# The gate columns of the first window of a hybrid decoder layer: projected third instead of eighth

## The chip, the core and the metric

The kernel runs on one core of a Trainium2 chip. The metric is the device time of one execution in microseconds (us). The engines are called as in the profile: PE (TensorE, the matrix engine; PEld is its weight loads), DVE (VectorE), ACT (ScalarE), POOL (GpSimd) and SP (SyncE, which here issues nearly all DMAs). Each engine runs its own instructions strictly in the order in which they stand; between engines, semaphores make one wait for another.

## What is computed

One layer on 2048 prompt tokens (one sequence) and 8 x 4 sample tokens, with D = 1024, in fp32:

```python
h = rms_norm(x, attn_norm)
u, q, k, v, g, z = split(h @ w_in)            # 512, 256, 256, 512, 512, 16 columns
y5 = rms_norm(GLU(gelu(S5(u))))               # 32 groups of complex diagonal state space
logf = log_sigmoid(z @ w_gate_up + b_gate) / 16
# gated linear attention, 4 heads, chunks of 64 tokens, b = cumsum(logf)
qe = q * exp(b); ke = k * exp(-b)
att = tril(qe @ ke.T); o = att @ v + qe @ S   # S: the state carried from chunk to chunk
o = rms_norm(o) * silu(g)
x = x + concat(y5, o) @ w_o
h2 = rms_norm(x); a, b = split(h2 @ w_up)     # 2 x 2816 columns
x = x + (silu(causal_conv3(a)) * b) @ w_down
```

Every fp32 product is made of three products of split values (high times high, high times low, low times high), so a block of 128 x 128 weights costs three matmuls per tile of tokens.

## The kernel before

**Stages.** The prompt goes through the first half of the layer in four windows of 512 tokens (`for w in range(NWIN)`); window 1 also carries the 32 sample tokens, so its tiles of columns are 272 wide. After the last window, the ConvFFN runs over all tokens. In the profile window 0 is the stretch from 20 to 212.4 us, windows 1 to 3 run to about 831, and the ConvFFN follows.

**A window.** First z (16 columns) is projected, and a generator `gen_gla_pre` (L1348) makes from it the decay factors: absolute value, exp and log on ACT, a subtraction and two scans on DVE (`TENSOR_TENSOR_SCAN`), subtractions of the value in the middle of each chunk, and then two exponentials on ACT, E1 = exp(b/16) and E2 = exp(-b/16), 128 x 1024 each (`qe` and `ke` in the code). Then the blocks of `w_in` follow in the order that `PARTS(w)` (L607) gives. A number is a block of 128 columns, done by `channels(m)` with columns on partitions and 512 tokens along the row: one PSUM bank, 24 matmuls. Blocks 0 to 3 are u (the bank is copied out by ACT), 4 and 5 are q, 6 and 7 are k. DVE multiplies q into E1 and k into E2 in place (`SCALAR_TENSOR_TENSOR t_L<-mm,t_L` and `TENSOR_TENSOR t_L<-mm,t_L`); at block 4 the builder first writes out the rest of `gen_gla_pre`. "v" and "g" are parts of 512 columns done by `tokens(part)` with tokens on partitions: four PSUM banks at once, one for each tile of 128 tokens, filled in four steps of 24 matmuls, one for each of four weight blocks. A tile of v is copied out, and with it the generator of the gated attention of these 128 tokens starts (`gen_gla_tile`); a tile of g goes through Silu on ACT and then through a product with a gain on POOL. After the part "g", two generators `gen_hT` for the next window are added as well: they load the next 512 rows of x, normalise them (ACT for the squares, DVE for `t_L<-t_L,rr,gain`), and, once all parts of this window are through, transpose and split them. At the end of a window come the products with `w_o` for the gated half of the mix: 2 halves of the columns times 4 tiles of 12 matmuls, each of which needs the attention's output of its tile.

**Banks.** PSUM's banks 0 to 3 (`mm` in the rows) serve these projections in turn, banks 4 to 7 (`bg`) the background work. A projection waits for the bank that it takes to be emptied.

**Weights.** A block of 512 KB is loaded by a DMA on SP's queue, its high part made by ACT (or POOL), its low part by POOL or DVE (`TENSOR_TENSOR t_L<-t_L,t_L 128x1024`). A list made from `PARTS` (`specs`, L611) sets the order of the loads.

**Order of the work.** The program is written out once, when it is built. All else than the projections is made of generators with priorities; a planner with a clock of estimated times writes out pieces of them between the groups of matmuls (`bg.tick()`), or until a given generator is done (`bg.drain`). Apart from the above, one such generator makes S5's tables (`gen_tables`): powers and products of complex numbers on DVE, first 16 x 128 to 16 x 512 elements, then eight tables with 16 products of 128 x 144 and 128 x 128 and two additions each. Another writes the first ConvFFN inputs at the end of window 3: rows of x are normalised, transposed by PE (`<-ident`), and evicted by ACT with a gain (`t_L<-bg,fgainc`). All instructions are recorded by one helper line (L290), so that the rows tell them apart by tiles: `mm`, `bg` and `all` are PSUM banks, `t_L`, `t_H` and `pair_L` slots of SBUF that serve all kinds of data, `decay` the decays of whole chunks, `rr` the reciprocal norms.

Of the kernel before, what the change touches and what calls it, by code (L numbers as in the profile page):

```python
# [29 lines left out]
NWIN = TP // WT  # L30
# [395 lines left out]
def kernel(ctx: ExitStack, tc: tile.TileContext, ins, outs):  # L426
# [179 lines left out]

    def PARTS(w):  # L607

        return (0, 1, 4, 5, 6, 7, "v", "g", 2, 3) if w < NWIN - 1 else (0, 1, 2, 3, 4, 5, 6, 7, "v", "g")

    specs = []  # L611
    swap = set()
    for w in range(NWIN):
        for part in PARTS(w):
            if isinstance(part, str):
                specs += [wrows(w_in, k, 1024 if part == "v" else 1536) for k in (0, 2, 4, 6)]
                continue
            if part < 4:
                swap.add(len(specs))
            specs.append(wcols(w_in, part * P))  # L620
        specs += [wrows(w_o, k, n * 512) for n in range(2) for k in (4, 6)]
# [1361 lines left out]
    for w in range(NWIN):  # L1983
# [100 lines left out]
        for part in PARTS(w):  # L2084
            if not isinstance(part, str):
                channels(part)
                continue
            if smp:
                BANKS.update(mm=(0, 5), bg=(5, 3))
            tokens(part)  # L2090
            if smp:
                BANKS.update(mm=(0, 4), bg=(4, 4))
                if part == "g":
                    S.put(xsamp.pop())
            if part == "g":
                if w + 1 < NWIN:
                    for pair in range(2):
                        hT[w + 1, pair] = bg.add(0, gen_hT(w + 1, pair))
                    if w + 1 == SW:
                        hT["s"] = bg.add(0, gen_hT_sample())  # L2100
# [610 lines left out]
```

## Time and profile before

| | |
|---|---|
| median of 3 runs | 2420.09 us (2413.03 to 2422.62) |
| the profiled execution | 2419.89 us, span 2418.2 us |
| mean granted clock of PE | 0.971 of full speed |
| PE busy | 2282.5 us (94%) |
| DVE busy | 1545.2 us (64%) |
| ACT busy | 896.8 us (37%) |
| POOL busy | 539.0 us (22%) |
| queue of the loads and stores | 357.53 MB, 47.0% of the 16 DMA engines |

Busy is the time in which an engine worked on an instruction; 94% for PE means that 135.7 us of the span are left in which no matmul ran. A share over the whole span does not tell where these are, so the rows below go by stretches and by waits.

### The profile page before, as it was taken

To read this page: it belongs to the slowest core of one execution; us is meant where nothing else is said; L and a number is where in the kernel's file an instruction comes from. 1 tells how busy PE (TensorE), PEld (TensorE's weight loads), DVE (VectorE), ACT (ScalarE), POOL (GpSimd) and SP (SyncE) were. 2 spreads that over 40 slices of the span, in tenths; PEclk is the share of its full clock that TensorE was granted. 3 is DMA by queue.
4 is the path that set the end of the run, shared out by engine and by line. 5 is a ranking of instruction groups with operands and counts; after the bars stand their busy time and mean duration, and the time that the engine had idled before them with its cause. 6 is when DMAs were issued, how large, how long until landed. Compare 5 with 4: busy or idle time off the path is not lost.

```text
span 2418.2 us, 32048 instructions
## 1 busy us (share of the span) xinstructions
PE 2282.5 (94%) x11809; PEld 1933.0 (80%) x11809; DVE 1545.2 (64%) x2743; ACT 896.8 (37%) x1634; POOL 539.0 (22%) x645
## 2 busy tenths in 40 slices
PE   7798999999999899999998998999999998999998
PEld 5577877777787689999998997887888776777776
DVE  6777547866633467654436655666666778686887
ACT  3243144434422453243233113344443435343444
POOL 5245425546432435631010010000000000000011
PEclk9899999999999999999999999999999999999999
DMA  6124546426653723344544752222222478676754
GB/s 170 62 94 132 149 121 196 115 83 200 174 168 112 252 93 106 114 143 121 168 166 142 249 177 62 68 81 87 79 79 79 147 232 267 226 247 215 242 184 151
DMA packets 357021, 359.72 MB, mean 149 GB/s; under 512 B 56546, under 2 KB 274842, under 8 KB 356864
## 3 DMA queue, kind: packets, MB, share of 16 engines
q1 hardware_dynamic: 356512, 357.53, 47.0%
q8 instruction: 93, 1.52, 0.3%
q14 instruction: 64, 0.52, 0.1%
q10 hardware_dynamic: 352, 0.15, 0.0%
HBM read 250.99 MB, written 106.62 MB: 148 GB/s over the span
## 4 chain that ended last, share of the span: by engine, by line
PE 61%; DVE 16%; ACT 6%; issue 4%; POOL 3%; DMA 1%; SPq 0%; ACTq 0%; DVEq 0%; POOLq 0%
PE all L290 42%; DVE t_L L290 13%; PE mm L290 11%; PE bg L290 8%; ACT t_L L290 5%; DVE t_H L290 2%; DVE pair_L L290 2%; POOL t_H L290 1%; POOL t_L L290 1%; POOL pair_L L290 1%; DMA t_L<-in_w_o_dram 0%; ACT t_H L290 0%; ACT pair_L L290 0%; DMA t_L<-Wd 0%; SPq L290 0%
## 5 line engine op out<-in xcount | busy, mean ns | idle before, releaser
L290 PE MATMUL all<-t_L,t_L 128*128 128x512 f32 (+4 forms) x7358 | 1472.2, 361 | 51.0 <-DVE t_L L290 20.0
L290 PEld LDWEIGHTS all<-t_L,t_L 128*128 128x128 f32 (+2 forms) x7358 | 1280.0, 189 | 236.4 <-DVE t_L L290 36.0
L290 DVE TENSOR_TENSOR t_L<-t_L,t_L 128x1024 fp32r<-128x1024 f32 (+9 forms) x636 | 553.0, 896 | 175.5 <-ACT t_L L290 116.3
L290 ACT ACTIVATE t_L<-t_L 128x1024 fp32r<-128x1024 f32 (+8 forms) x450 | 361.9, 825 | 440.8 <-DVE t_L L290 360.3
L290 PE MATMUL mm<-t_L,t_L 128*128 128x512 f32 (+2 forms) x2160 | 491.5, 384 | 15.4 <-DVE t_L L290 12.3
L290 PEld LDWEIGHTS mm<-t_L,t_L 128*128 128x128 f32 (+1 forms) x2160 | 382.6, 191 | 100.5 <-issue 17.5
L290 POOL TENSOR_SCALAR rr<-ss 128x1 f32<-128x1 f32 (+1 forms) x51 | 19.7, 386 | 1044.7 <-ACT pair_L L290 955.2
L290 DVE TENSOR_TENSOR t_L<-t_L,all 128x512 f32<-128x512 f32 (+2 forms) x268 | 172.4, 643 | 101.8 <-PE all L290 37.9
L290 POOL TENSOR_SCALAR t_L<-t_L 128x1024 fp32r<-128x1024 f32 (+1 forms) x91 | 117.4, 1298 | 320.5 <-PE all L290 146.7
L290 POOL TENSOR_TENSOR t_L<-t_L,t_L 128x1024 fp32r<-128x1024 f32 x49 | 136.3, 2784 | 51.8 <-ACT t_L L290 39.6
L290 ACT ACTIVATE t_L<-all 128x512 f32<-128x512 f32 (+2 forms) x134 | 71.6, 539 | 191.0 <-PE all L290 186.1
L290 DVE TENSOR_TENSOR t_L<-t_L,pair_L 128x512 f32<-128x512 f32 (+2 forms) x138 | 93.4, 679 | 56.4 <-ACT pair_L L290 51.4
L290 ACT ACTIVATE pair_L<-all 128x512 f32<-128x512 f32 (+1 forms) x104 | 61.6, 593 | 154.1 <-PE all L290 134.1
L290 PE MATMUL bg<-t_L,t_L 128*128 128x256 f32 (+7 forms) x628 | 111.2, 344 | 2.3 <-DVE t_H L290 2.3
L290 DVE SCALAR_TENSOR_TENSOR t_L<-all,cw,t_L 128x351 f32<-128x351 f32 (+1 forms) x132 | 74.7, 566 | 48.0 <-ACT t_L L290 47.2
L290 PEld LDWEIGHTS bg<-t_L,t_L 128*128 128x128 f32 (+4 forms) x628 | 85.1, 183 | 24.6 <-issue 10.8
L290 ACT ACTIVATE t_L<-all,cw 128x352 f32<-128x352 f32 x66 | 42.4, 642 | 147.1 <-PE all L290 130.2
L290 ACT ACTIVATE t_L<-bg 128x512 fp32r<-128x512 f32 (+7 forms) x121 | 53.5, 461 | 103.8 <-PE bg L290 99.3
L290 DVE SCALAR_TENSOR_TENSOR t_L<-t_L,cw,t_L 128x1024 f32<-128x1024 f32 x44 | 56.5, 1285 | 24.6 <-ACT t_L L290 23.8
L290 ACT ACTIVATE junk<-bg 128x128 bf16<-128x128 f32 (+1 forms) x68 | 18.8, 276 | 120.5 <-PE bg L290 118.9
L290 ACT ACT_TABLE_LOAD x41 | 52.6, 1283 | 23.0 <-DVE t_L L290 14.7
L290 DVE TENSOR_TENSOR t_L<-pair_L,t_L 128x144 f32<-128x144 f32 (+5 forms) x107 | 54.6, 538 | 8.2 <-ACT pair_L L290 5.8
(180 smaller groups left out, 1643.4 us busy)
## 6 DMA issues: line engine op xcount, KB each, us to landing
t_L<-in_w_up_dram SPq DMA_DIRECT2D x88, 512.0 KB, 4.9
t_L<-x2d SPq DMA_DIRECT2D x80, 512.0 KB, 5.9
t_L<-in_w_in_dram SPq DMA_DIRECT2D x64, 512.0 KB, 5.5
x2d<-t_L SPq DMA_DIRECT2D x48, 512.0 KB, 3.1
gT<-t_L SPq DMA_DIRECT2D x44, 512.0 KB, 2.7
t_L<-gT SPq DMA_DIRECT2D x48, 384.0 KB, 4.8
t_L<-in_w_down_dram SPq DMA_DIRECT2D x34, 512.0 KB, 4.9
t_L<-in_w_o_dram SPq DMA_DIRECT2D x24, 512.0 KB, 5.5
```

Of the source, the lines that this page charges most:

```text
L290: r = fn(*args, **kw)
```

## The change

`PARTS` gives window 0 an order of its own: "g" stands third, behind the u blocks 0 and 1, instead of eighth. Windows 1 to 3 keep theirs.

```diff
     def PARTS(w):

-        return (0, 1, 4, 5, 6, 7, "v", "g", 2, 3) if w < NWIN - 1 else (0, 1, 2, 3, 4, 5, 6, 7, "v", "g")
+        return (0, 1, "g", 4, 5, 6, 7, "v", 2, 3) if w == 0 else (0, 1, 4, 5, 6, 7, "v", "g", 2, 3) if w < NWIN - 1 else (0, 1, 2, 3, 4, 5, 6, 7, "v", "g")
```

The matmuls stay the same. The weight loads follow the new order, the two generators for window 1's rows are added after the third part instead of the eighth, and the planner, whose clock now sees other waits, writes out the background work at other places all through the first third of the program. Three places show it.

ACT, in window 0, around E1 and E2. Before (`t_L_453` and `t_L_454` are E1 and E2, `t_L_319` one of S5's 16-partition arrays, `decay_412` the decays):

```order
L290 ACTIVATE decay_412<-decay_412 128x16
L290 ACTIVATE t_L_319<-t_L_319 16x128
L290 ACT_TABLE_LOAD
L290 ACTIVATE t_L_319<-t_L_319 16x128 x2
L290 ACT_TABLE_LOAD
L290 ACTIVATE t_L_453<-t_L_409 128x1024
L290 ACTIVATE t_L_454<-t_L_409 128x1024
L290 ACTIVATE t_L_633<-t_L_585 128x1024
```

With the change (E1 and E2 are `t_L_480` and `t_L_481`, and `mm_403` to `mm_406` are g's four tiles):

```order
L290 ACTIVATE decay_439<-decay_439 128x16
L290 ACTIVATE t_L_480<-t_L_436 128x1024
L290 ACTIVATE t_L_481<-t_L_436 128x1024
L290 ACTIVATE t_L_319<-t_L_319 16x128
L290 ACT_TABLE_LOAD
L290 ACTIVATE t_L_319<-t_L_319 16x128 x2
L290 ACT_TABLE_LOAD
L290 ACTIVATE pair_L_557<-mm_403 128x512
L290 ACTIVATE pair_L_557<-mm_404 128x512
L290 ACTIVATE pair_L_580<-mm_405 128x512
L290 ACTIVATE pair_L_580<-mm_406 128x512
L290 ACTIVATE t_L_599<-t_L_545 128x1024
```

E1 and E2 moved up before S5's operations, and the four Silus stand behind all of them; the first matmul of block 4 waits for the first Silu, since it takes that bank.

DVE, where blocks 4 to 7 are multiplied into E1 and E2. Before (`mm_457`, `mm_489`, `mm_521`, `mm_553` are the four blocks):

```order
L290 SCALAR_TENSOR_TENSOR t_L_453<-mm_457,t_L_453 128x512
L290 SCALAR_TENSOR_TENSOR t_L_453<-mm_489,t_L_453 128x512
L290 TENSOR_TENSOR t_L_454<-mm_521,t_L_454 128x512
L290 TENSOR_TENSOR t_L_454<-mm_553,t_L_454 128x512
L290 TENSOR_TENSOR pair_L_437<-t_L_432 16x128
```

With the change (`mm_603`, `mm_677`, `mm_722`, `mm_762`; the rows with `rr` are normalisations of window 1's rows, those of 16 partitions S5's tables, of which the first and the last of a run are shown):

```order
L290 TENSOR_TENSOR t_L_513<-t_H_517,pair_L_320 16x512
L290 SCALAR_TENSOR_TENSOR t_L_480<-mm_603,t_L_480 128x512
L290 SCALAR_TENSOR_TENSOR t_L_616<-t_L_616,rr_622,gain 128x1024
...
L290 SCALAR_TENSOR_TENSOR t_L_480<-mm_677,t_L_480 128x512
L290 COPY t_L_514<-t_L_512 16x128
...
L290 SCALAR_TENSOR_TENSOR t_L_626<-t_L_626,rr_667,gain 128x1024
L290 TENSOR_TENSOR t_L_481<-mm_722,t_L_481 128x512
L290 TENSOR_TENSOR t_H_517<-t_L_514 16x256
...
L290 TENSOR_TENSOR t_L_515<-t_H_517,pair_L_320 16x512
L290 TENSOR_TENSOR t_L_481<-mm_762,t_L_481 128x512
```

The four products stood together and are now spread: three normalisations between the first two, eight operations on S5's arrays and two normalisations between the second and the third, twelve operations on S5's arrays between the third and the last. The first of the four also stands behind a whole block of S5's operations that it stood ahead of before.

PE, at the end of window 3, where the `w_o` products end and the ConvFFN begins. Before (`bg` and `all` rows are transposes of the first ConvFFN inputs, `all_7073` the first FFN product):

```order
L290 MATMUL mm_6916<-t_L_6815,t_L_6719 128x512
L290 MATMUL bg_6932<-ident,t_L_6767 128x128 x4
L290 MATMUL bg_6945<-ident,t_L_6767 128x128 x4
L290 MATMUL bg_6984<-ident,t_L_6769 128x128 x4
L290 MATMUL bg_6997<-ident,t_L_6769 128x128 x4
L290 MATMUL all_7045<-ident,t_L_6771 128x128 x4
L290 MATMUL all_7058<-ident,t_L_6771 128x128 x4
L290 MATMUL all_7073<-t_L_6734,t_L_6821 128x352
```

With the change, two pieces with 30 matmuls between them (`mm_6828`, `mm_6948` and `mm_7001` are `w_o` products):

```order
L290 MATMUL mm_6828<-t_L_6612,t_L_6726 128x512
L290 MATMUL bg_6844<-ident,t_L_6789 128x128 x4
L290 MATMUL bg_6857<-ident,t_L_6789 128x128 x4
L290 MATMUL mm_6897<-t_L_6660,t_L_6688 128x512
...
L290 MATMUL mm_6948<-t_L_6883,t_L_6718 128x512
L290 MATMUL bg_6963<-ident,t_L_6791 128x128 x4
L290 MATMUL bg_6976<-ident,t_L_6791 128x128 x4
L290 MATMUL mm_7001<-t_L_6660,t_L_6726 128x512
```

The transposes of the first two tiles moved in between the last `w_o` products; all of them stood behind the last of these before.

## Rows read from the trace of the kernel before

**Rows 1.** The page's first part: busy us, share of the span, instructions.
```profile
PE 2282.5 (94%) x11809; PEld 1933.0 (80%) x11809; DVE 1545.2 (64%) x2743; ACT 896.8 (37%) x1634; POOL 539.0 (22%) x645
```
**Rows 2.** Stretches: length, busy us of PE, PEld, DVE, ACT, POOL (instructions), PE clock, DMA share, GB/s.
```profile
100.00:140.00 40.00, 37.82 (x207) 28.25 (x205) 12.20 (x45) 7.61 (x32) 6.02 (x7) 0.83 0.15 53
831.00:848.00 17.00, 5.71 (x28) 4.16 (x26) 7.62 (x21) 15.90 (x38) 7.37 (x12) 0.64 1.03 356
20.00:212.40 192.40, 165.42 (x762) 127.37 (x761) 142.62 (x266) 60.32 (x114) 83.87 (x58) 0.88 0.35 101
212.40:831.00 618.60, 596.06 (x3294) 475.30 (x3293) 354.45 (x672) 226.50 (x508) 265.75 (x277) 0.97 0.51 151
```
**Rows 3.** Waits of PE from 20 to 212.4 us: total us, times, longest us.
```profile
PE bg L290 <- DVE pair_L L290: 11.8, 2, 8.2
PE mm L290 <- DVE t_L L290: 10.7, 1, 10.7
```
**Rows 4.** PE's timeline in window 0: start, us, operation, count, [idle before <-releaser].
```profile
44.62 16.51 PE L290 MATMUL mm<-t_L,t_L 128*128 128x512 f32 x70 [1.25 <-POOL t_L L290]
...
71.84 22.53 PE L290 MATMUL mm<-t_L,t_L 128*128 128x512 f32 x84 [10.71 <-DVE t_L L290]
...
104.85 0.49 PE L290 MATMUL bg<-t_H,t_H 128*128 128x128 f32 x2 [2.18 <-DVE t_H L290]
...
157.68 2.79 PE L290 MATMUL bg<-ident,pair_L 128*128 128x128 f32 x12 [3.59 <-DVE pair_L L290]
...
203.01 1.09 PE L290 MATMUL bg<-ident,pair_L 128*128 128x128 f32 x4 [8.23 <-DVE pair_L L290]
```
**Rows 5.** ACT's timeline in window 0.
```profile
64.52 0.31 ACT L290 ACTIVATE t_L<-t_L 16x128 f32<-16x128 f32 x1 [7.95 <-DVE t_L L290]
64.84 1.28 ACT L290 ACT_TABLE_LOAD   x1
...
66.66 1.28 ACT L290 ACT_TABLE_LOAD   x1
67.96 4.85 ACT L290 ACTIVATE t_L<-t_L 128x1024 f32<-128x1024 f32 x5
...
147.26 0.60 ACT L290 ACTIVATE t_H<-mm 128x512 f32<-128x512 f32 x1
```
**Rows 6.** DVE's timeline in window 0 and the first microseconds of window 1.
```profile
58.65 4.26 DVE L290 TENSOR_TENSOR t_L<-t_L,pair_L 128x512 f32<-128x512 f32 x2
...
71.03 1.27 DVE L290 SCALAR_TENSOR_TENSOR t_L<-mm,t_L 128x512 f32<-128x512 f32 x2
...
73.42 4.78 DVE L290 TENSOR_TENSOR pair_L<-t_L 16x128 f32<-16x128 f32 x2
...
82.28 0.75 DVE L290 TENSOR_TENSOR pair_L<-t_L 16x256 f32<-16x256 f32 x2
...
88.08 0.68 DVE L290 TENSOR_TENSOR t_L<-pair_L 16x512 f32<-16x512 f32 x1
...
88.96 0.47 DVE L290 TENSOR_TENSOR pair_L<-t_L 16x128 f32<-16x128 f32 x2
...
171.71 4.86 DVE L290 SCALAR_TENSOR_TENSOR t_L<-t_L,rr,gain 128x1024 f32<-128x1024 f32 x4
...
189.88 1.30 DVE L290 TENSOR_TENSOR t_L<-pair_L,t_L 128x144 f32<-128x144 f32 x2
...
213.17 0.52 DVE L290 TENSOR_TENSOR t_L<-pair_L,t_L 128x144 f32<-128x144 f32 x2
...
217.20 0.69 DVE L290 TENSOR_TENSOR t_H<-t_H,t_H 128x512 f32<-128x512 f32 x1
```
**Rows 7.** POOL's timeline beside DVE's block from 73.42: low parts of weights.
```profile
70.98 7.07 POOL L290 TENSOR_TENSOR t_L<-t_L,t_L 128x1024 fp32r<-128x1024 f32 x3 [8.61 <-ACT t_L L290]
```
**Rows 8.** PE's timeline where the ConvFFN begins.
```profile
835.36 1.59 PE L290 MATMUL bg<-ident,t_L 128*128 128x128 f32 x8 [2.86 <-ACT t_L L290]
...
842.60 1.97 PE L290 MATMUL all<-ident,t_L 128*128 128x128 f32 x8 [5.65 <-ACT t_L L290]
```

## The prediction, made before the changed kernel was run

> **What bounds the kernel now.** I read five views, from coarse to fine. The page's first part says that TensorE (PE) is busy for 2282.5 of the span's 2418.2 us [rows 1]: a change that only reorders can win back PE's idle time and nothing else, so I look for idle time that this change can reach. The table of stretches gives it: the first window of 512 tokens (20 to 212.4 us) has 192.40 - 165.42 = 27.0 us without PE work, while the three other windows together (212.4 to 831 us) have 618.60 - 596.06 = 22.5 us in more than three times the length [rows 2]. The waits of PE in the first window name who ends that idle time, and VectorE (DVE) ends nearly all of it: 10.7 us once before a projection, 11.8 us in two waits of the output side [rows 3]. PE's timeline places them [rows 4]. The first projections end at 44.62 + 16.51 = 61.13; the next matmul starts at 71.84, 10.71 us later, on a DVE release. Smaller waits follow at 104.85 (2.18) and 157.68 (3.59), and a larger one at 203.01 (8.23). Window 1 begins at 212.4.
>
> The wait at 61 is this one. Block 4 (q) is multiplied by the decay factors E1, block 6 (k) by E2; until DVE has done that, the four banks stay full, and "v", the next part, needs all four. DVE reads E1 and E2 at 71.03 [rows 6]; ScalarE (ACT) has made them in the five operations from 67.96, behind one 16x128 operation at 64.52 and two table loads [rows 5]. So PE stands behind a chain DVE scan, DVE subtractions (58.65, ended at 62.9), ACT, DVE.
>
> **The change, part by part** (+ is time lost; the sum is made against the profiled execution, 2419.89 us, which lies 0.2 us under the median of 2420.09).
>
> (a) *Removed: the wait before v.* Parts 0, 1 and "g" together have as many matmuls as 0, 1, 4, 5, 6, 7, so PE still runs without a pause to 61.13, and the next thing it meets is now block 4, not v. Block 4 needs an empty bank only, not E1. **-10.7**. With it goes the 2.18 wait at 104.85, on the first tile of the gated attention, which v now feeds later: **-2.2**.
>
> (b) *Added: block 4 waits for g's first bank.* g's four banks are emptied by Silu on ACT, and the order shows Silu behind E1, E2, the 16x128 operations and two table loads. DVE's subtractions end at 62.9 [rows 6]; E1 and E2 take 4.85 / 5 = 0.97 each [rows 5], to 64.85; then the operations and table loads that take from 64.52 to 66.66 + 1.28 = 67.94, 3.4 us, to 68.2; the first Silu takes 0.60 [rows 5], to 68.8. PE waits from 61.1 to 68.8: **+7.7**. Bounds: 6 if one table load overlaps the subtractions' end, 9.5 if the small DVE operations that feed the 16x128 ones slip by 2 us. On this the Trainium skill speaks against the change: "ScalarE: Activation LUTs", section What ACT_TABLE_LOAD costs, puts 1.28 us of load and some 1.38 us of drain on each switch of table. By it two switches would hold Silu 2.8 us longer, the wait would be 10.5 and the whole sum below -1.1. The rows do not show the drain: the load at 66.66 is followed by work at 67.96, right at its end [rows 5], so I keep 7.7.
>
> (c) *Added: v waits for blocks 4 to 7 all the same, later.* Before, DVE does their four products back to back at 71.03. Now each waits for its own matmuls, and the order puts between them a block of the S5 tables' 16-partition operations, twelve more of them later, and the five normalisations of window 1's rows, which come early because "g" sets them free. When is the last of the four done? Blocks 4 to 7 are 96 matmuls, 22.53 / 84 = 0.268 us each just after a pause [rows 4], so they run from 68.8 to 94.5, and v's fourth tile wants its bank 18 matmuls later, at 99.4. The first table block took from 73.42 to 88.08 + 0.68 = 88.76 before, 15.3 us [rows 6]; now it starts at 71, with a weight subtraction of about 1.2 in it, so DVE comes to block 4's product at 87.5. A product takes 1.27 / 2 = 0.63, a normalisation 4.86 / 4 = 1.2 [rows 6]: block 4's is done at 88.1, three normalisations at 91.7, block 5's at 92.3, eight small operations (0.47 / 2 each, 1.9) and two normalisations at 96.6, block 6's at 97.3, twelve table operations (as from 82.28 to 88.76, 6.5 [rows 6]) at 103.8, block 7's at 104.4. PE waits 104.4 - 99.4 = **+5.0**. Bounds: 0 if the first table block runs undisturbed (its 16x128 pair then takes 0.47 instead of 4.78 [rows 6]), 12 if the normalisations and the second block run at the disturbed price.
>
> At about 105, then, PE has lost 7.7 + 5.0 where it lost 10.7 + 2.2: the sum of (a) to (c) is **-0.2**. The wait is not removed; it is cut in two, one part behind ACT and one behind DVE.
>
> (d) *The end of the first window.* Before: 3.59 + 8.23 and under 1 us more, 12.7 [rows 4]. The 8.23 is a gated output that stands on DVE behind one S5 table of 18 operations, from 189.88 until PE goes on at 203.01, 13.1 us, while the same table takes 4.7 us from 213.17 to 217.89 [rows 6]. The change does not take a table from in front of the output: the new order has such a table ahead of the third output tile again, and one table more finished before window 1's gates. Before, DVE was busy for 12.20 of the 40 us from 100 to 140 [rows 2], room to work off a backlog, but v's tiles now come last, with blocks 2 and 3 alone to cover them. I take 9 us behind the table (between 4.7 and 13.1, nearer the disturbed price, since POOL still makes weights there) and 3 elsewhere: 12 for 12.7, **-0.7**. Bounds -8 and +8: no table in the way, or two at the full price.
>
> (e) *Windows 1 to 3.* Same parts in the same order; other background work falls beside them. PE's idle time there is 22.5 us in all, and one S5 table more or less moves between windows: **0**, bounds -5 and +5.
>
> (f) *Into the ConvFFN.* Before, PE waits for ACT twice while the first FFN rows are scaled, transposed and evicted, 2.86 and 5.65 us [rows 8], at a granted clock of 0.64 over the stretch [rows 2]. In the order after the change, the transposes of the first two tiles stand among the last output products, which cover one such round: **-3**, bounds 0 and -8.5 (both waits).
>
> Moved at no price: the loads of window 1's rows on the SP queue, ahead of v's weights now; in the first window DMA is busy for 0.35 of the time [rows 2], and weights come two blocks ahead. If that cover were gone, v's first matmul would come a block's load later, a few us, inside (c)'s bounds.
>
> Sum: -0.2 - 0.7 + 0 - 3 = **-3.9**, so 2419.89 - 3.9 = **2416.0 us**. The bounds do not all fall together; added as independent they make about 11 to either side: 2405 to 2427.
>
> **The rivals.**
> - *The waits really go (faster).* If DVE runs its table blocks undisturbed, (c) is 0 and (d) comes out at -8; with both waits of (f), which are 8.5, the sum is -0.2 - 5.0 - 8 - 8.5 = -21.7, **about 2398**; with one of the last two halved, some 2403. For it: DVE's 28 idle us from 100 to 140, and tables done early. Against it: POOL makes half the weights' low parts throughout, and the table blocks seen beside that are slow. Chance 0.23.
> - *DVE's backlog decides (slower).* Five normalisations and a table more at the disturbed price: (c) at 12 instead of 5.0, (d) at +8 and (f) at 0, together -0.2 + 7.0 + 8 = +14.8, **about 2435**. It decides from the point where block 7's product lands later than 99.4. For it: 13.1 against 4.7 us for one table, and POOL's three weight subtractions, 7.07 us, over the slow 16x128 pair [rows 4, 6, 7]. The "GPSIMD Engine Reference", section 1 Specifications, in the Trainium skill names a shared SBUF interface with such two-input DVE work, and this pair (4.78 beside POOL, 0.47 without) agrees. Against it: the work is the same in sum, and that idle time takes some of it. Chance 0.12.
> - *Nothing comes of it.* The cut wait costs what it saved, and the early transposes only move ACT's chain: (f) 0, **2419 to 2420**. Chance 0.2; it lies in the forecast's own range.
>
> **How the numbers follow.** Forecast 0.45, and the three rivals as given. A change of 0.5%, 12 us, is about what a measurement of this kernel can tell from none. Below 2408 lie the faster rival's 0.23 and a tenth of the forecast: 0.28. Above 2432 lies nearly all of the slower rival's 0.12: 0.11. Within: 0.61. Half of the faster rival lies below 2400 (0.12) and two thirds of the slower one above 2431 (0.08), so the range that leaves out 2 in 10 is 2400 to 2431.
>
> **What would show it.** In PE's timeline after: no pause at 61 that ends on DVE, but one of 6 to 9.5 us that ends on ACT before block 4; a second of 0 to 12 us on DVE between 94 and 105; window 1 starting within 8 us of 212.4; the first 352-wide matmul some 3 us sooner relative to the last output product. Wrong would be: no pause at 61 at all (E1 before Silu is then not the chain), a window 1 that starts before 202 (the waits went) or after 222 (backlog), or a difference that arises only after 900 us, where the order hardly changes.

## The result, and the profile after

The changed kernel takes 2438.22 us (median of 4 runs, 2435.81 to 2443.30), the kernel before 2421.36 us in the runs beside it: ratio 1.0078, 95% interval 1.0054 to 1.0102. It is slower, by 13 to 25 us; 2416.0 was predicted, with a range that ended at 2431. The profiled execution took 2435.81 us, 15.9 more than the one of before.

The page's first part, after, answers to [rows 1]:

```profile
PE 2281.7 (94%) x11809; PEld 1928.6 (79%) x11809; DVE 1529.0 (63%) x2730; ACT 907.9 (37%) x1651; POOL 508.8 (21%) x642
```

PE has done the same work in 0.8 us less; all that was lost is idle time. So the first view to read is the table of stretches, cut where each window's first matmul starts and where the first 352-wide matmul of the ConvFFN does: length, busy us of PE, PEld, DVE, ACT, POOL (instructions), PE clock, DMA share, GB/s. Before (windows 0 to 3, then the ConvFFN):

```profile
20.17:212.36 192.19, 165.21 (x760) 127.16 (x759) 142.45 (x266) 60.15 (x114) 83.87 (x58) 0.88 0.35 101
212.36:409.14 196.78, 192.39 (x1227) 158.42 (x1226) 117.56 (x259) 68.33 (x174) 78.24 (x61) 0.98 0.55 154
409.14:604.31 195.17, 183.01 (x959) 140.64 (x958) 134.51 (x272) 87.06 (x197) 106.11 (x154) 0.95 0.45 132
604.31:847.00 242.69, 225.75 (x1140) 180.15 (x1138) 109.75 (x162) 86.01 (x172) 88.76 (x74) 0.96 0.56 177
847.00:2418.20 1571.20, 1509.04 (x7701) 1320.19 (x7701) 1029.38 (x1771) 585.41 (x964) 172.21 (x283) 0.98 0.47 151
```

With the change:

```profile
19.86:219.13 199.27, 167.17 (x775) 126.89 (x774) 149.41 (x306) 58.03 (x116) 73.83 (x53) 0.88 0.37 103
219.13:427.68 208.55, 192.35 (x1198) 157.68 (x1196) 116.47 (x242) 68.27 (x174) 85.27 (x82) 0.96 0.52 149
427.68:643.93 216.25, 199.13 (x1073) 154.41 (x1071) 132.93 (x265) 100.63 (x213) 94.38 (x140) 0.94 0.43 128
643.93:867.77 223.84, 213.65 (x1049) 168.61 (x1047) 97.11 (x152) 86.90 (x164) 69.87 (x60) 0.98 0.53 165
867.77:2433.70 1565.93, 1502.73 (x7693) 1315.39 (x7693) 1021.94 (x1754) 584.10 (x971) 175.53 (x292) 0.99 0.48 153
```

Length less PE's busy time is the idle time, before and after: window 0 27.0 and 32.1 us (+5.1), window 1 4.4 and 16.2 (+11.8), window 2 12.2 and 17.1 (+5.0), window 3 with the way into the ConvFFN 16.9 and 10.2 (-6.8), ConvFFN 62.2 and 63.2 (+1.0). Of the 22.9 us that were lost (6.8 came back in window 3), 16.8 arise in windows 1 and 2, whose own order of parts was not changed.

PE's timeline of window 0 after, its pauses of over 2 us and the small ones before v (start, us, operation, count, [idle before <-releaser]):

```profile
64.32 24.93 PE L290 MATMUL mm<-t_L,t_L 128*128 128x512 f32 x96 [4.13 <-ACT pair_L L290]
91.56 1.63 PE L290 MATMUL mm<-t_L,t_L 128*128 128x512 f32 x6 [2.31 <-DVE t_L L290]
99.88 2.93 PE L290 MATMUL mm<-t_L,t_L 128*128 128x512 f32 x6 [6.69 <-DVE t_L L290]
104.69 2.93 PE L290 MATMUL mm<-t_L,t_L 128*128 128x512 f32 x6 [1.88 <-DVE t_L L290]
111.69 9.84 PE L290 MATMUL mm<-t_L,t_L 128*128 128x512 f32 x30 [4.08 <-DVE t_L L290]
...
196.80 4.63 PE L290 MATMUL mm<-t_L,t_L 128*128 128x512 f32 x10 [10.17 <-DVE t_L L290]
```

The single wait of 10.71 us [rows 4] is gone. In its place stand 4.13 us before block 4, on ACT, and one wait before each of v's four tiles, 2.31 + 6.69 + 1.88 + 4.08 = 15.0 us, on DVE. Each of these tiles wants the bank of one of the blocks 4 to 7. DVE's timeline after shows why they are full:

```profile
56.92 1.29 DVE L290 TENSOR_TENSOR t_L<-t_L,pair_L 128x512 f32<-128x512 f32 x2
...
79.50 2.89 DVE L290 TENSOR_TENSOR t_L<-t_H,pair_L 16x512 f32<-16x512 f32 x1
82.42 2.78 DVE L290 TENSOR_TENSOR t_H<-t_L,t_L 16x512 f32<-16x512 f32 x1
85.14 2.89 DVE L290 TENSOR_TENSOR pair_L<-t_L,t_L 16x512 f32<-16x512 f32 x1
88.06 2.75 DVE L290 TENSOR_TENSOR t_L<-t_H,pair_L 16x512 f32<-16x512 f32 x1
90.74 0.67 DVE L290 SCALAR_TENSOR_TENSOR t_L<-mm,t_L 128x512 f32<-128x512 f32 x1
91.34 7.88 DVE L290 SCALAR_TENSOR_TENSOR t_L<-t_L,rr,gain 128x1024 f32<-128x1024 f32 x3
...
110.96 0.67 DVE L290 TENSOR_TENSOR t_L<-mm,t_L 128x512 f32<-128x512 f32 x1
```

Block 4's 24 matmuls, a quarter of the 96 from 64.32, were through at about 71; its product comes at 90.74, block 7's at 110.96. The same 16x512 operation takes 0.68 [rows 6] and 2.8 here, a normalisation 1.2 [rows 6] and 7.88 / 3 = 2.6. POOL's timeline beside it, to be read against [rows 7]:

```profile
79.43 10.82 POOL L290 TENSOR_TENSOR t_L<-t_L,t_L 128x1024 fp32r<-128x1024 f32 x4 [0.76 <-ACT t_L L290]
90.34 3.01 POOL L290 TENSOR_SCALAR t_L<-t_L 128x1024 fp32r<-128x1024 f32 x1
93.44 3.51 POOL L290 TENSOR_TENSOR t_L<-t_L,t_L 128x1024 fp32r<-128x1024 f32 x1
```

Four subtractions of POOL take 10.82 us, and four operations of DVE beside them 11.3: about one of the one for one of the other. ACT's timeline after, where E1, E2 (with the 16-partition operation, the first row) and g's Silus (the last) follow one another:

```profile
58.25 2.20 ACT L290 ACTIVATE t_L<-t_L 128x1024 f32<-128x1024 f32 x3 [3.42 <-DVE t_L L290]
60.47 1.28 ACT L290 ACT_TABLE_LOAD   x1
61.76 0.51 ACT L290 ACTIVATE t_L<-t_L 16x128 f32<-16x128 f32 x2
62.29 1.28 ACT L290 ACT_TABLE_LOAD   x1
63.58 2.06 ACT L290 ACTIVATE pair_L<-mm 128x512 f32<-128x512 f32 x4
```

Window 1's cost sits at its end. DVE's timeline before: the clearing at 363.37 is made by the first of S5's scans, the four normalisations are those of window 2's rows.

```profile
363.37 0.11 DVE L290 MEMSET t_L<- 64x64 f32 x1
...
370.35 5.73 DVE L290 SCALAR_TENSOR_TENSOR t_L<-t_L,rr,gain 128x1024 f32<-128x1024 f32 x4
```

The same after, and PE's timeline where it then waits for the transposes of these rows and for their split:

```profile
318.53 0.18 DVE L290 MEMSET t_L<- 64x64 f32 x2
...
412.97 5.37 DVE L290 SCALAR_TENSOR_TENSOR t_L<-t_L,rr,gain 128x1024 f32<-128x1024 f32 x2
...
424.44 3.58 PE L290 MATMUL bg<-ident,t_L 128*128 128x128 f32 x16 [3.59 <-DVE t_L L290]
...
431.56 1.06 PE L290 MATMUL mm<-t_L,wz 128*32 128x512 f32 x2 [2.33 <-DVE t_L L290]
```

S5's tables are done earlier, so two scans start 45 us earlier, side by side and ahead of window 2's rows, which are normalised 43 us later (window 1 itself began 7 us later). And on the way into the ConvFFN the three waits on the first inputs, to be read against [rows 8], are small now:

```profile
863.33 1.09 PE L290 MATMUL bg<-ident,t_L 128*128 128x128 f32 x8 [0.39 <-ACT t_L L290]
864.72 0.63 PE L290 MATMUL bg<-ident,t_L 128*128 128x128 f32 x4 [0.30 <-DVE t_L L290]
865.66 0.66 PE L290 MATMUL bg<-ident,t_L 128*128 128x128 f32 x4 [0.31 <-DVE t_L L290]
```

### The profile page after: what moved, and what is told of

Same layout as the page of the kernel before. It is cut to its first block, busy times and chain, and to the rows that moved or that the text cites. A ratio compares the mean times of both kernels' runs of the same rounds, so it can differ in the third digit from the quotient of the medians.

```text
span 2433.7 us, 31995 instructions
## 1 busy us (share of the span) xinstructions
PE 2281.7 (94%) x11809; PEld 1928.6 (79%) x11809; DVE 1529.0 (63%) x2730; ACT 907.9 (37%) x1651; POOL 508.8 (21%) x642
## 4 chain that ended last, share of the span: by engine, by line
PE 50%; DVE 13%; ACT 7%; issue 4%; POOL 2%; DMA 1%; SPq 0%; POOLq 0%; DVEq 0%; ACTq 0%
PE all L290 41%; DVE t_L L290 11%; ACT t_L L290 6%; PE bg L290 5%; PE mm L290 4%; DVE t_H L290 1%; POOL t_H L290 1%; POOL t_L L290 1%; ACT t_H L290 0%; ACT pair_L L290 0%; DVE pair_L L290 0%; DMA t_L<-Wd 0%; POOL pair_L L290 0%; ACT L290 0%; DMA t_H<-in_x_prompt_dram 0%
## 5 line engine op out<-in xcount | busy, mean ns | idle before, releaser
L290 DVE TENSOR_TENSOR t_L<-t_L,t_L 128x1024 fp32r<-128x1024 f32 (+8 forms) x645 | 570.4, 910 | 198.9 <-ACT t_L L290 142.2
L290 PE MATMUL mm<-t_L,t_L 128*128 128x512 f32 (+2 forms) x2160 | 503.2, 389 | 43.1 <-DVE t_L L290 32.5
L290 POOL TENSOR_SCALAR rr<-ss 128x1 f32<-128x1 f32 (+1 forms) x51 | 15.4, 302 | 1057.0 <-ACT pair_L L290 957.2
L290 POOL TENSOR_SCALAR t_L<-t_L 128x1024 fp32r<-128x1024 f32 (+1 forms) x85 | 107.6, 1273 | 360.2 <-PE all L290 160.8
L290 DVE TENSOR_TENSOR t_L<-t_L,pair_L 128x512 f32<-128x512 f32 (+3 forms) x130 | 85.7, 662 | 74.1 <-ACT pair_L L290 52.5
L290 POOL TENSOR_TENSOR t_L<-t_L,t_L 128x1024 fp32r<-128x1024 f32 x40 | 110.9, 2776 | 27.0 <-ACT t_L L290 21.0
L290 PE MATMUL bg<-t_L,t_L 128*128 128x512 f32 (+8 forms) x628 | 108.5, 336 | 2.9 <-DVE t_L L290 2.1
L290 PEld LDWEIGHTS bg<-t_L,t_L 128*128 128x128 f32 (+5 forms) x628 | 82.9, 178 | 25.1 <-issue 7.7
L290 ACT ACTIVATE t_L<-bg 128x512 fp32r<-128x512 f32 (+6 forms) x121 | 53.0, 461 | 117.0 <-PE bg L290 114.3
L290 POOL TENSOR_TENSOR t_H<-t_H,t_L 128x128 f32<-128x128 f32 (+5 forms) x114 | 55.1, 503 | 72.9 <-DVE t_L L290 32.6
L290 ACT ACT_TABLE_LOAD x42 | 53.9, 1283 | 16.5 <-DVE t_L L290 11.2
L290 DVE SCALAR_TENSOR_TENSOR t_L<-t_L,rr,gain 128x1024 f32<-128x1024 f32 (+1 forms) x34 | 51.7, 1537 | 12.7 <-POOL rr L290 6.5
```

The source lines that it names most:

```text
L290: r = fn(*args, **kw)
```

## The experiments

Idle times are lengths less PE's busy times in a run's own table of stretches, cut as above; they come from the one profiled execution of each run, the totals are medians. The theory after the two traces: in window 0, DVE's other work in front of the four products costs the 15.0 us, and POOL beside it makes that work long; in windows 1 and 2, the scans that start earlier cost the rest. Rivals: the normalisations that "g" sets free early; the mere amount of DVE work, whatever POOL does; the delay of window 0 itself.

**Which work of DVE?** Window 1's rows set free behind v:

```diff
-            if part == "g":
+            if part == ("v" if w == 0 else "g"):
                 if w + 1 < NWIN:
                     for pair in range(2):
                         hT[w + 1, pair] = bg.add(0, gen_hT(w + 1, pair))
```

> The change, but the generators of window 1's rows are added behind v, as the eighth part, so that no normalisation stands between the products of blocks 4 to 7; S5's table operations move up in their place (14, 6 and 24 of them between the four products instead of 0, 8 and 12). In the changed kernel the pauses of PE before v's four tiles are 2.3 + 6.7 + 1.9 + 4.1 = 15.0 us, and the normalisations took 7.88 + 2.46 = 10.3 us of DVE. If the normalisations are the cause, the pauses fall to 5 us or less. If any DVE work queued there is the cause, the tables take their place and the pauses stay at 9 us or more.

Measured: 2442.00 us, ratio 1.0099 (1.0078 to 1.0119). The pauses before v's tiles are 0.95 + 3.15 + 1.62 + 5.46 = 11.2 us, and one of 5.07 has come up within blocks 4 to 7. The normalisations alone are not the cause; the tables took their place. Window 0's idle time falls to 26.4, window 1's is 17.5.

The tables held back until v is through:

```diff
     def gen_first():
+        while "v0" not in flags:
+            yield "idle"
         yield from gen_tables()
...
             tokens(part)
+            if part == "v":
+                flags.add("v0")
```

> The change, but S5's tables are held back until v of window 0 is through, so that only the five normalisations and low parts of weights stand between the four products. If the backlog of table operations ahead of block 4's product is the cause (16 x 512 operations of 2.8 us), the pauses before v's tiles fall from 15.0 to 5 us or less, and the pause before block 4 too may shrink, since no sine stands ahead of Silu (4.1 to 3 or less). If the normalisations are, they stay at 8 or more. The tables come later, so the end of window 0 or window 1 may lose what this gains: window 1 then starts no earlier than 215.

Measured: 2504.59 us, ratio 1.0357 (1.0329 to 1.0385). There is no pause of PE from 40 to 150 us, neither before v nor before block 4, although the five normalisations are still there. So the table operations are what matters ahead of the products, though not they alone were taken away: in this order POOL makes one low part between 60 and 110 us, where it makes six with the change. Window 1 starts at 186.3, where no earlier than 215 was expected; that was wrong. The price comes later: window 1 is idle for 22.9 us, window 2 for 41.7 and window 3 for 36.6 (16.2, 17.1 and 10.2 with the change), while the ConvFFN stays at 62.1. Late tables are dear.

**POOL or the amount of work?** DVE alone makes the low parts in window 0:

```diff
-    W.ring, W.hi_pool, W.lo_eng = 3, False, [G, V]
+    W.ring, W.hi_pool, W.lo_eng = 3, False, [V]
...
         S.put(st["qe"], st["ke"])
+        W.lo_eng = [G, V]
```

> The change, but in window 0 DVE alone makes the low parts of the weights, so that POOL does no 1024-wide subtraction beside DVE. If what slows DVE is POOL's work beside it (16 x 512 operations at 2.8 instead of 0.68 us, normalisations at 2.6 instead of 1.2), DVE's operations there go back to 0.68 and 1.2, and the pauses before v's tiles fall from 15.0 to 5 us or less although DVE has more to do. If the amount of work is the cause, they stay at 10 or more.

Measured: 2418.54 us, ratio 0.9991 (0.9979 to 1.0004). Of the pauses before v's tiles 0.87 us is left, on the fourth; before block 4 there is none, and 0.27 within blocks 4 to 7. DVE has four more subtractions in the stretch and still comes to block 4's product at 71.36 instead of 90.74. Window 0 is idle for 13.2 us and 29 us shorter; 10 us of the 29 are PE's busy time, 27 matmuls that moved to window 1 and, for the smaller part, a higher mean granted clock (0.95; 0.88 with the change). Windows 1 and 2 stay at 16.6 and 18.0 idle.

That run reorders the work too. This one does not: on every engine each instruction stands where it stood, and only POOL's operation is another. The low parts are left out: zeros stand in their place.

```diff
-            sub(lv, rv, f(hv), eng)
+            if eng is G and self.made < 20:
+                G.e.tensor_scalar(lv, rv, 0.0, None, op0=ALU.mult)
...
+            else:
+                sub(lv, rv, f(hv), eng)
```

> The change with every instruction in the same place on every engine, but POOL's share of window 0's low parts of weights (14 subtractions of two inputs, 2.4 us each undisturbed) is made by an operation of one input that writes zeros (1.05 us): this kernel leaves out those low parts. In the changed kernel four DVE operations of 16 x 512 elements take 2.8 us each while POOL makes four low parts at 2.7 us each, and then 0.68. If a DVE operation that meets one of POOL's has to wait for it, each shrinks with POOL's, to 1.0 to 1.9 us, and the pauses before v's tiles fall from 15.0 to 9 us or less. If the amount of DVE work in the queue is the cause, they stay at 13 or more.

Measured: 2429.23 us, ratio to before 1.0034 (1.0017 to 1.0051), 9 us under the changed kernel. DVE's timeline of this run, and POOL's beside it:

```profile
74.12 0.67 DVE L290 TENSOR_TENSOR pair_L<-t_L 16x512 f32<-16x512 f32 x1
74.83 1.41 DVE L290 TENSOR_TENSOR t_L<-t_H,pair_L 16x512 f32<-16x512 f32 x1
76.27 0.68 DVE L290 TENSOR_TENSOR t_H<-t_L,t_L 16x512 f32<-16x512 f32 x1
...
79.52 4.43 DVE L290 SCALAR_TENSOR_TENSOR t_L<-t_L,rr,gain 128x1024 f32<-128x1024 f32 x3
...
74.58 12.02 POOL L679 TENSOR_SCALAR t_L<-t_L 128x1024 fp32r<-128x1024 f32 x4
```

POOL's operation did not get shorter, it takes 12.02 / 4 = 3.0 us instead of 2.7; yet DVE's beside it take 0.67 to 1.41 instead of 2.8. So it is not only how long POOL works that holds DVE up; the form of what it does counts, two inputs against one. One input is not free either: in this run two of DVE's 16x256 operations, at 89.54 and 90.98, took 1.51 and 1.25 us instead of 0.41 while POOL's one-input operations went on. PE's two remaining pauses before v, and the row of window 0:

```profile
89.67 1.67 PE L290 MATMUL mm<-t_L,t_L 128*128 128x512 f32 x6 [2.29 <-DVE t_L L290]
98.62 8.63 PE L290 MATMUL mm<-t_L,t_L 128*128 128x512 f32 x30 [7.29 <-DVE t_L L290]
...
19.94:203.28 183.34, 158.59 (x777) 121.16 (x775) 135.23 (x305) 58.24 (x116) 78.92 (x53) 0.94 0.40 111
```

9.6 us, just over the 9 that the theory allowed: block 7's product comes 13 us earlier, at 97.9 instead of 111.0, but PE is there earlier too, since block 4 waits 0.52 us instead of 4.13. A pause of 1.30 us has come up within blocks 4 to 7. Both causes are real: 9.6 us of the pauses stay with DVE's queue beside one-input work of POOL, the other 5.4, and 3.6 before block 4, are the price of POOL's two inputs. The total does not follow from the pauses alone. Window 0 is 15.9 us shorter, 7.3 of it idle time and 8.6 in the same matmuls, at a mean granted clock of 0.94 instead of 0.88; the later stretches lose 9 of the 15.9 again, 6.9 of them in the ConvFFN's matmuls (1509.65 us busy instead of 1502.73, at 0.98 instead of 0.99). Whether zeros among the weights have a part in the clock was not separated.

**The scans.** Held to the end of window 1:

```diff
         yield from gen_tables()
+        while "w1" not in flags:
+            yield "idle"
         flags.add("tables")
```

> The change, but S5's scans may start only when window 1 is written out to its end; window 0 stays as it is with the change (idle 32 us). In the changed kernel PE is idle for 16.2 us in window 1 where it was 4.4 before, and 17.1 in window 2 where it was 12.2. If S5's scans, started earlier by the earlier tables, are what fills DVE, POOL and the slots at the end of window 1, its idle time falls to 7 us or less and window 3 gets longer. If it is the delay of window 0 and the later loads of window 2's rows, window 1 stays at 12 us or more.

Measured: 2472.17 us, ratio 1.0225 (1.0207 to 1.0243). Window 1's idle time falls to 6.7 and window 2's to 13.2, with a window 0 (33.6 idle) that is as late as before: the scans are the cause there, not the delay. But held so long they cost window 3 its gain and more: 42.6 us idle up to the first 352-wide matmul (10.2 with the change), and 62.9 in the ConvFFN, as before.

Held until window 2's rows are loaded (the same wait, on a flag that `gen_hT(2, 1)` sets when its loads are written out):

> The change, but S5's first scans may start only when the loads of window 2's rows have been written out; window 0 stays as with the change (idle 32 us). In the changed kernel those rows' normalisations come at 413 us, PE waits 3.6 us for their transposes and 2.3 us for their splits, and DMA is busy for 0.08 of 340 to 380 us. If the scans cost window 1 its idle time by taking the slots of SBUF that the rows and the weights need, window 1's idle time falls from 16.2 to 9 us or less and the scans still come early. If it is their work on DVE and POOL, it stays at 12 us or more.

Measured: 2459.93 us, ratio 1.0176 (1.0144 to 1.0207). Window 1 is at 5.5 us, window 2 at 14.1, but window 3 is idle for 29.7 us and the ConvFFN for 73.7. Half of the expectation failed: the first scan starts at 355, 37 us later than with the change. That is still 8 us earlier than in the kernel before, whose window 3 and ConvFFN are idle for 16.9 and 62.2, so its start alone does not explain the price; the cause of that stays open.

One scan let through, the others after the loads:

```diff
-        while live[0] >= s5_width[0] or S.open() < 6.5 or (hf and not X2L):
+        while live[0] >= s5_width[0] or S.open() < 6.5 or (hf and not X2L) or (live[0] >= 1 and "rows2" not in flags):
             yield "idle"
```

> The change, but of S5's scans in window 1 only one may start before the loads of window 2's rows are written out (two do in the changed kernel, at 318 us, and the rows are normalised at 413; before, one does, at 363, and the rows are normalised at 370). Window 0 stays (idle 32 us). If the second scan is what keeps the rows out, window 1's idle time falls from 16.2 to 8 us or less, window 2's from 17.1 to 14 or less, and since scans are not held for long, the ConvFFN stays at 62 to 64 us idle (73.7 where all scans waited): in total 5 to 12 us under the changed kernel. If it is one scan's work on DVE and POOL already, window 1 stays at 12 or more.

Measured: 2430.04 us, ratio 1.0040 (1.0025 to 1.0056), 8 us under the changed kernel. Window 1's row of the stretches, DVE's clearing and first normalisation, and PE's waits on the way into the ConvFFN:

```profile
216.27:415.05 198.78, 191.14 (x1213) 157.06 (x1212) 107.40 (x224) 69.80 (x174) 72.23 (x66) 0.98 0.54 153
...
315.78 0.11 DVE L290 MEMSET t_L<- 64x64 f32 x1
...
367.20 1.27 DVE L290 SCALAR_TENSOR_TENSOR t_L<-t_L,rr,gain 128x1024 f32<-128x1024 f32 x1
...
842.79 1.53 PE L290 MATMUL bg<-ident,t_L 128*128 128x128 f32 x8 [2.87 <-ACT t_L L290]
...
850.04 1.97 PE L290 MATMUL all<-ident,t_L 128*128 128x128 f32 x8 [5.71 <-ACT t_L L290]
```

7.6 us idle, window 2 at 9.9, the ConvFFN at 62.8. One scan at 316 us does no harm in windows 1 and 2; the second, ahead of the rows, does. But window 3 goes from 10.2 to 17.4 us idle: the two waits on ACT of [rows 8] are back, though the order of window 0 is the changed one. What the second early scan costs in windows 1 and 2 it gives back in part at the entry of the ConvFFN, which is why 15.8 us less idle time in windows 1 and 2 make only 8 in the total.

**Is it the place of g at all?** The kernel before with the low parts on DVE in window 0 (the edit shown above):

> The kernel before with the one edit that took the pauses out of the changed kernel: in window 0 DVE alone makes the low parts of the weights. If the wait of 10.7 us before v and the 8.2 us at the end of window 0 are longer for POOL's work beside DVE (the two subtractions at 58.65 took 4.26 us where the changed kernel's took 1.29), window 0's idle time falls from 27 to 20 us or less. If E1's chain through ACT is the whole of the 10.7 us, only the 8.2 us shrink, and idle time stays at 21 or more. The total is at or below that of the changed kernel with this edit (2418.5 us) if the order of the parts has no worth of its own.

Measured: 2431.05 us, ratio 1.0048 (1.0026 to 1.0069): worse than without. Window 0's wait before v is 9.88 us (10.71 before), its idle time 26.3; window 1 goes to 17.8, because the tables are early and two scans start at 308. Of the expectation only the 21 or more held: the wait before v stayed, and in place of 3.59 and 8.23 stand 5.52, 5.84 and 4.96. Beside the changed kernel with the same edit (2418.54, window 0 idle for 13.2) this is the one pair in which g third is the faster, by 12 us, all of it in window 0. Window 3 shows the same exchange as with the change, 11.8 us idle, with waits of 0.40 and 0.32 at the entry of the ConvFFN, and here g stands eighth. The same with one scan held as well (here until the rows are normalised):

> The kernel before with both edits of the last one: the control for what the place of g is worth when neither POOL's subtractions nor the early scans are in its way. Window 0 stays at 26 us idle (as with the first edit alone, 2431 us). If the early scans cost window 1 here too (17.8 us idle), it falls to 8 or less, and the total to 2418 to 2425: then the place of g is worth 10 us or more once the two costs are gone. If the total comes to within 4 us of the changed kernel's with both edits, the place of g is worth nothing.

Measured: 2419.97 us, ratio 1.0003 (0.9988 to 1.0017). Window 1 falls to 7.9 us, the total by 11. The early second scan costs the old order about as much as the new one (8 us). The changed kernel with these two edits:

> The change with DVE alone making the low parts in window 0, and only one of S5's scans started in window 1 before window 2's rows are normalised (two start together at 364 us without this, the rows are normalised at 390, and PE waits 8.5 us there). Window 0 stays at 13 us idle. If the two scans together are what cost window 1 its 16.6 us, it falls to 8 or less and the total from 2418.5 to 2403 to 2412. If not, both stay.

Measured: 2440.42 us, ratio 1.0074 (1.0048 to 1.0100). This missed: it is 20 us over the old order with the same edits; window 1 is at 13.7, window 3 goes to 26.0. In this order the rows are normalised at 387 us with one scan and at 390 with two, so another thing keeps them late. What it is was not found.

The two causes of the changed kernel taken away together, in the order of the run with one scan:

> The change with POOL's low parts of window 0 made by an operation of one input that writes zeros (as in the run before this; those low parts are left out), and with only one scan of window 1 before window 2's rows are loaded; all instructions stand as in the run with one scan alone (2430 us). If the two causes are independent, their 9 and 8 us add: 2438 - 17 = 2421 us, within 4, no slower than the kernel before; window 0 idle 25 us or less and window 1 idle 8 us or less in the same run. If they are two sides of one thing, the total stays at 2427 or more.

Measured: 2415.75 us, ratio 0.9990 (0.9973 to 1.0007). The two add, and a little more: 22 us under the changed kernel, 1 us more than the range that the theory gave. Window 0 is idle for 23.5 us, window 1 for 7.6. And the control, the kernel before with POOL's operation of one input:

> The kernel before with POOL's 16 low parts of window 0 made by the same operation of one input (they are left out), every instruction in its place. If POOL's two-input work costs the order before as much as the changed one, window 0 gets shorter by 10 to 16 us (192.2 us before) and the total by 8 or more. If the changed order suffers more, because four of DVE's 16 x 512 operations and five normalisations meet POOL ahead of products that PE waits for, window 0 gains 8 us or less here and the total 5 or less.

Measured: 2396.31 us, ratio 0.9911 (0.9876 to 0.9945). The wait before v is 5.63 us, the one of 8.23 at the end of window 0 is gone, and window 0's idle time is 11.5 us; it is 21.8 us shorter, more than the 10 to 16 of the first alternative. So the second alternative is wrong: POOL's two-input work costs the old order more (24 us, of which some 14 are idle time and 10 the matmuls, at a mean granted clock of 0.95 in window 0 instead of 0.88) than the new one (9 us). It is a cost that both pay, and without it the change is not better but worse: 2429 against 2396, and 2416 against 2396 with the second scan held as well. So these two costs are not all that sets the orders apart: some 20 us are left, 12 of them idle time in window 0 (23.5 against 11.5). Nor has the place of g a worth of its own that holds everywhere: in window 0 the changed order is idle for 5 us more than the old one as the kernels stand, for 13 less when DVE makes the low parts, and for 13 more when POOL's operation has one input (24.8 against 11.5). (The two are not quite alike: at the end of window 0 the changed kernel's table still meets one of POOL's subtractions, for window 1's weights, and six one-input operations just before it, and its wait of 10.17 us stays.)

**Another order.** With a third u block ahead of q and k:

```diff
-        return (0, 1, "g", 4, 5, 6, 7, "v", 2, 3) if w == 0 else
+        return (0, 1, 2, 4, 5, 6, 7, "v", "g", 3) if w == 0 else
```

> Another order for window 0: 0, 1, 2, 4, 5, 6, 7, v, g, 3. A block of u, whose bank ACT empties without waiting for E1, covers the chain to E1 with 24 more matmuls (6 us), and no Silu comes early. If the wait before v (10.7 us) is E1's chain alone, it falls to 5 us or less and nothing is put between the four products. If DVE's backlog sets it, it stays at 8 or more, behind other work.

Measured: 2433.20 us, ratio 1.0068 (1.0043 to 1.0093). The wait before v is 6.52 us, between the two alternatives, and another of 4.18 follows, since some of S5's operations came between the third and the fourth product after all; window 1 goes to 18.1, with two scans at 312. With the low parts on DVE in window 0:

> The same order, with the low parts of the weights made by DVE alone in window 0. If POOL's work beside DVE is what remains of the wait before v, it is gone here (1 us or less), and window 0's idle time is 15 us or less; the total is then the lowest so far, below 2415 us, unless windows 1 and 2 give it back as in the changed kernel with the same edit (16.6 and 18.0 us idle).

Measured: 2404.27 us (2399.41 to 2406.70), ratio 0.9938 (0.9915 to 0.9960): faster than both kernels, with the whole computation. Its windows 0 to 2:

```profile
19.87:194.49 174.62, 159.23 (x759) 123.76 (x758) 132.78 (x292) 58.45 (x112) 41.05 (x42) 0.93 0.38 104
194.49:390.31 195.82, 191.44 (x1227) 157.37 (x1226) 119.29 (x253) 68.23 (x174) 75.36 (x59) 0.99 0.57 160
390.31:587.25 196.94, 184.11 (x960) 141.07 (x958) 134.29 (x272) 87.19 (x197) 107.24 (x156) 0.95 0.44 131
```

The gain is all in window 0 (15.4 us idle, and it starts window 1 18 us earlier), and windows 1 and 2 keep their 4.4 and 12.8 us: here one scan starts 7 us before the rows are normalised, as in the kernel before. The wait before v is still 5.98 us, not 1 or less, though POOL makes no low parts there. ACT has made both E1 and E2 by 62.34; DVE comes to the first product at 64.26, behind S5's small operations, and PE goes on at 66.12, when DVE has also made a low part (64.86 to 66.06).

## Why the prediction was wrong, step by step

(a) Right: the wait of 10.71 us went, and the one of 2.18 with it.

(b) The mechanism was right, the size not: 4.1 us for 7.7, under the lower bound of 6. DVE came to its two subtractions 1.7 us earlier, and POOL was idle at that time, so they took 1.29 us instead of the 4.26 of [rows 6]. The first Silu starts at 63.58, right at the end of the load from 62.29; the 1.38 us of drain which the Trainium skill ("ScalarE: Activation LUTs", What ACT_TABLE_LOAD costs) adds to each switch do not show here either.

(c) This step failed: 15.0 us for 5.0, above the bound of 12. DVE came to block 4's product at 90.7, not 87.5; the three normalisations took 7.88 us, not the 3.6 of a price read where POOL made almost no weights; so block 7's product was done at 111.6 instead of 104.4. And PE was ready earlier, mostly by what (b) had gained: blocks 4 to 7 ended at 89.25, not 94.5. The step had put the whole disturbance on the first table block, at the price that it had had before, and none on the normalisations; the wait that it saw on v's fourth tile alone came in four parts. The run with POOL's one-input operation leaves 9.6 of the 15.0 us. With (a) and (b) the sum is 4.1 + 15.0 - 10.7 - 2.2 = +6.2, for -0.2.

(d) Right: 1.5 + 1.1 + 10.2 and 0.25 us against 12.7; the 10.2 is again a product that stands behind one S5 table.

(e) This step failed too, and it is the largest: 0 with bounds of 5 was predicted, and windows 1 and 2 lost 11.8 + 5.0. "One S5 table more or less moves between windows" was priced as work that moves. What moved with it was the start of what waits for the tables: two scans that take slots of SBUF and time on DVE and POOL before the rows of the next window are in. The run with one scan shows it: 16.2 to 7.6 us in window 1, 17.1 to 9.9 in window 2, 8 us in all. How much of that is slots and how much is work was not separated.

(f) Within the bounds, but partly by luck: the waits on ACT of 2.86 and 5.65 [rows 8] became 0.39 + 0.30 + 0.31, so -7.5 for -3. The step took this for a gain of its own. The runs show it as the other side of (e): with one scan the waits are 2.87 and 5.71 again, and the old order has the gain too when two scans start early (0.40 and 0.32). Taken together, (e) and (f) were forecast at -3 and came to about +10.

The sum of the bounds was a little narrow as well: added as independent they make 12 to 13 us to either side, not 11. 2438 lies outside of either.

The rival "DVE's backlog decides" gave 2435 with the place (c), which came, and with a second late table in (d), which did not. Its time was near for half the reason; it was given 0.12, and its price in (c), 12 us, was the upper bound that I had worked out and not believed. "GPSIMD Engine Reference", section 1 (Specifications), in the Trainium skill names the conflict of POOL with DVE's two-input operations. The rows agree (2.8 us beside POOL's subtractions, 0.68 without), and in the run with POOL's one-input operation the loss was smaller, 0.7 us at most on a 16x512 operation.

## What to carry to other kernels

A wait that is removed by reordering is paid for by whatever the new order puts in front of the instruction that frees the buffer: write down that engine's queue between the old and the new place, and price each entry as it runs beside its new neighbours, not as it ran alone. Where a planner places background work, ask which later work it releases: what came early in window 0 cost most in window 1. And look for the cost that both orders share: here POOL's subtractions beside DVE cost the kernel before 24 us, as the run without them shows, more than the 10.7 us of the wait that the change was about.

## What was unexpected of the hardware

DVE's 16x512 operations of two inputs took 2.8 us beside POOL's 128x1024 subtractions (2.7 us each) and 0.67 to 1.41 beside POOL's one-input operations, though these were as long (2.8 to 3.0 us). That one-input operation, a multiplication alone, took 2.78 us at 40.08, while DVE was idle, and the kernel's own (a multiplication and an addition, same shape and type) takes 1.05. DVE in turn holds up POOL: a one-input copy there took 4.32 us beside DVE's normalisations and table operations.
